# Two gate projections of the short convolution, moved from dense jobs into two groups of seven block products

## The chip, the core and the metric

The kernel runs on one core of one Trainium2 chip: one launch, with inputs and outputs in DRAM. The metric is the device time of the whole program in microseconds (us). TensorE (PE) multiplies, VectorE (DVE) and ScalarE (ACT) do elementwise work, GpSimd (POOL) does a little elementwise work and issues some transfers, SyncE (SP) issues most transfers. PEld is TensorE's weight load, which runs beside the matmuls.

## What is computed

One hybrid decoder layer over 1024 tokens with 16 meta tokens in front, width 1024, all in float32. Three causal mixers read the same normalised stream `xn` through one wide projection `w_in`; this is the reference, cut to what matters here:

```
xn   = rms_norm(x, norm_pre)
proj = xn @ w_in                      # split into ssd_*, sc_b, sc_c, sc_h, sc_g, dn_*, gate_logits
y_sc = sc_b * causal_depthwise_conv(sc_c * sc_h, sc_conv_w) * silu(sc_g)     # 3 taps
branch = einsum("btnw,nwd->btnd", [y_ssd, y_sc, y_dn], w_branch)
merged = sum over the 3 branches of sigmoid(gate_logits) * branch
out  = x + rms_norm(merged @ w_out, norm_post)
```

The change is about `sc_g` and `sc_b`, each a 1024 x 1024 x 1024 product followed by an elementwise multiplication.

## The kernel before

Activations lie with channels on the 128 partitions and tokens along the free dimension. Every float32 operand of a product is split into a high and a low part (ACT casts, DVE subtracts), and each product is three matmuls: high by high, high by low, low by high.

**Mixing stage.** 84 *dense jobs* each compute 128 output channels of `w_in` for all tokens: 8 blocks of k, three matmuls each, for two groups of 512 tokens (48 matmuls) or, where the result goes into a convolution, three groups of some 345 (72 matmuls). A job loads 512 KB of weights and splits them one job ahead (`split`, lines 159 to 167). Beside the jobs run the *mixes*: eight heads of the DeltaNet (`dn_mix`, tiles dm0 to dm7), whose last part is a chain over nine chunks in which every chunk takes three dependent steps (a matmul ks, then DVE's R; a matmul pn, then ACT's vn; a matmul su, then DVE's new state S), then eight pairs of SSD heads (`sd_mix`, tiles sm0 to sm7). Each mix is one *slot*; `weave` (line 192) hands out dense matmuls between the steps of a mix, `want * gap` columns of them, with a gap per kind of slot from the table `GAPS`, and then finishes the slot's jobs. A scheduler in the language then orders each engine's instructions. A DeltaNet slot holds the four jobs of the next head (q, k, v, z) and some jobs of the short convolution. The latter are four per 128 channels (`sc_jobs`, line 741): c and h (three groups each, then the three taps on DVE), g (SiLU on ACT, a multiplication on DVE) and bb (a multiplication on DVE, then stores of the rows to DRAM). The eight DeltaNet slots take 4, 3, 4, 3, 4, 4, 2 and 4 of these 32 jobs, and the last SSD slot ("sl") takes the last four. The last SSD slot also ends the row norm of the SSD branch: a matmul with the mean matrix (tiles sm7ms), a square root on ACT, a reciprocal of one row on DVE (line 908) and a store of that row (`rin_d`, line 909).

**Product stage.** The square products left are done by Strassen's scheme in Winograd's form: seven products of halves (512 x 512 x 512, 48 matmuls each, lines 1136 to 1138) in place of eight. A *group* is one such product, a *phase* one of its seven; phases are numbered n = 0 to 48 over seven groups (gate and branch for each of the three mixers, in the order 2, 1, 0, then the output). PSUM banks y and z hold the running sums; `finish` (line 1155) does the elementwise end of each quarter: a sigmoid for a gate group; a multiplication with the gate, and but for the first branch an addition to `merged`, for a branch group. For the next phase, each phase loads operand halves (`tr`), splits them into th and tl, and splits the weights w. The seven right operands of each product are sums of quarters that lie ready in DRAM; POOL makes them with accumulating transfers (`sums`, line 125), issued one by one, with a small copy (`tick`, line 1247) as a marker of the phase. `scale_tasks` (line 1218) applies the SSD row norm: it loads pieces `ys`, DVE multiplies them by the row `rin` (line 1232), and they are stored. In before its loads are on SP's queue and its stores on ACT's.

Order of work around the change: each engine works strictly in the order in which its instructions stand, and an instruction that waits holds everything behind it on that engine.

Of the kernel before, what the change touches and what calls it, by code (L numbers as in the profile page):

```python
# [12 lines left out]
ALU = mybir.AluOpType  # L13
# [26 lines left out]
GAPS = {"sm": 1.0, 8: 2.3, 7: 2.0, 6: 1.75, "s0": 2.0, "sd": 2.4, "sx": 2.0, "sg": 2.0, "sl": 2.6}  # L40
# [43 lines left out]
def hybrid_block(  # L84
# [40 lines left out]
    def sums(s, straight=None, ks=slice(0, HK)):  # L125

        o = {n: t[:, ks, :] for n, t in dict(opd[s], **(straight or {})).items()}
# [613 lines left out]
    def sc_jobs(t):  # L741
        n = f"sc{t}"
        tl = {}
        h0 = META - 2

        def c(w):
            tl["c"] = tmp(n + "c")
            yield from dense(w, xh, xl, three(h0), lambda o, c0, m: A.copy(tl["c"][:, c0:c0 + m], o), name=n + "c")

        def hh(w):  # L750
            ch = tl["c"]
            yield from dense(w, xh, xl, three(h0),
                             lambda o, c0, m: V.tensor_tensor(ch[:, c0:c0 + m], o, ch[:, c0:c0 + m], ALU.mult),
                             name=n + "h")
            acc = tl["a"] = big(n + "a", "sca", 1, SEQ)
            V.tensor_scalar(acc, ch[:, h0:h0 + SEQ], sc_cw(0, t), None, ALU.mult)
            for k in range(1, 3):
                V.scalar_tensor_tensor(acc, ch[:, h0 + k:h0 + k + SEQ], sc_cw(k, t), acc, ALU.mult, ALU.add)

        def g(w):  # L760
            gs = tmp(n + "g")
            yield from act_job(gs, n + "g")(w)
            V.tensor_tensor(tl["a"], tl["a"], gs[:, :SEQ], ALU.mult)

        def bb(w):
            acc = tl["a"]

            def use(o, c0, m):
                s = acc[:, c0 - META:c0 - META + m]
                j = (c0 - META) // HALF  # L770
# [205 lines left out]
    late = (lambda: (yield from chain(lambda: sums("dn"), lambda: sums("sc", ks=slice(0, HK - 1)))))()  # L976

    slot("dn", None, lambda: dn_jobs(0, dnt[0]))
    for h, n in enumerate((4, 3, 4, 3, 4, 4, 2, 4)):
        fs = [lambda h=h: dn_jobs(h + 1, dnt[h + 1])] if h < DN_H - 1 else [  # L980
            lambda: sdg_jobs(0, grps[0]), lambda: sd_jobs(0, sdt[0])]
        slot(4 + n, lambda h=h: beside(lambda: dn_mix(h, dnt[h]), early, 9), lambda n=n: sc_next(n), *fs)
    for t in range(KT):
# [3 lines left out]
        mix = lambda gens=gens: beside(lambda: chain(*gens), late, 7)  # L987
# [3 lines left out]
        fs.append((lambda t=t: sd_jobs(t + 1, sdt[t + 1])) if t < KT - 1 else lambda: sc_next(4))  # L991
# [163 lines left out]
    def finish(g, i, j, u):  # L1155
# [62 lines left out]
    def scale_tasks():  # L1218
        for i in range(2):
            for j in range(2):  # L1220
# [29 lines left out]

    g0 = groups[0]
# [7 lines left out]
    for n, (g, ph) in enumerate(steps):  # L1259
# [75 lines left out]
```

## Time and profile before

| | us |
|---|---|
| median of 3 runs (lowest, highest) | 1863.25 (1862.57, 1865.03) |
| profiled execution, its own time | 1867.32 |
| its span, first to last instruction | 1865.2 |
| PE busy / DVE busy / ACT busy / POOL busy | 1822.1 / 1272.1 / 829.4 / 200.4 |
| mean granted TensorE clock | 0.992 of full speed |

The profile is one execution. Matmuls overlap in the pipeline, so that the duration of one (some 390 ns at 512 columns) is longer than the distance from one start to the next; what a matmul costs the stream is that distance. "Idle before" is the time an engine stood still ahead of an instruction, with what ended it. A window of the profile gives each engine's busy time and the granted clock in a stretch.

### The profile page before, as it was taken

How to read it: one execution, taken by the hardware profiler on the slowest of the kernel's cores; microseconds unless marked ns; L12 is line 12 of the kernel's file. 1: busy time of each engine (PE TensorE's matmuls, PEld its weight loads, DVE VectorE, ACT ScalarE, POOL GpSimd, SP SyncE). 2: the span in 40 equal slices, each digit the busy share in tenths (PEclk: the TensorE clock that was granted, in tenths of full speed). 3: DMA queues.
4: the chain of work that ended last, by engine and by line, in shares of the span. 5: the costliest groups of instructions: out<-in, count | busy, mean ns of one | idle time of the engine just before them, and what ended most of it. 6: DMA issues, size and time to landing. Idle time of an engine off the chain costs nothing.

```text
span 1865.2 us, 27616 instructions
## 1 busy us (share of the span) xinstructions
PE 1822.1 (98%) x11115; PEld 1576.5 (85%) x11115; DVE 1272.1 (68%) x1874; ACT 829.4 (44%) x1343; POOL 200.4 (11%) x339
## 2 busy tenths in 40 slices
PE   6999999999999999999999999999989999999997
PEld 5988988888888889888888899888777888888886
DVE  5576674656766666575756887786757857867787
ACT  5442524344352342434334556453535455455454
POOL 3011112010120100101001121110000000000000
PEclk8999999999999999999999999999999999999999
DMA  5123244233342311111124465222776545755532
GB/s 154 49 68 118 76 104 112 68 114 102 91 108 63 91 52 41 46 58 46 40 75 112 127 147 150 78 80 94 248 249 212 155 164 144 232 184 158 192 102 91
DMA packets 153482, 214.23 MB, mean 115 GB/s; under 512 B 11169, under 2 KB 97374, under 8 KB 153226
## 3 DMA queue, kind: packets, MB, share of 16 engines
q1 hardware_dynamic: 135666, 160.02, 27.3%
q0 software_dynamic: 11632, 32.51, 8.5%
q10 hardware_dynamic: 6056, 19.93, 2.7%
q8 instruction: 87, 1.43, 0.3%
q14 instruction: 41, 0.34, 0.1%
HBM read 179.83 MB, written 64.07 MB: 131 GB/s over the span
## 4 chain that ended last, share of the span: by engine, by line
PE 86%; DVE 5%; DMA 4%; ACT 2%; issue 1%; POOL 1%; SPq 0%; DVEq 0%; ACTq 0%; POOLq 0%
PE py L1138 5%; PE py L1137 5%; PE py L1136 5%; PE pz L1138 4%; PE pz L1137 3%; PE pz L1136 3%; DMA ys<-y_sd 1%; DMA a__13752<-in_w_branch_dram 1%; DVE gt L1214 1%; DVE w L163 0%; DMA gain<-in_norm_pre_dram 0%; DMA sd_n<-ys 0%; DMA tr<-dn_n 0%; DVE dm7osq L734 0%; DMA x_t<-x_t 0%
## 5 line engine op out<-in xcount | busy, mean ns | idle before, releaser
L1138 PE MATMUL py<-th,w 128*128 128x512 f32 x432 | 168.9, 391 | 3.8 <-DVE w L1117 3.6
L1136 PE MATMUL py<-th,w 128*128 128x512 f32 x432 | 168.8, 391 | 0.0
L1137 PE MATMUL py<-tl,w 128*128 128x512 f32 x432 | 168.8, 391 | 0.0
L1101 DVE TENSOR_TENSOR tl<-tr,th 128x1024 fp32r<-128x1024 f32 x94 | 114.0, 1221 | 66.2 <-ACT th L1100 65.5
L1100 ACT CAST th<-tr 128x1024 fp32r<-128x1024 f32 x94 | 98.4, 1053 | 105.8 <-PE py L1138 44.2
L1138 PE MATMUL pz<-th,w 128*128 128x512 f32 x320 | 124.8, 390 | 3.5 <-DVE w L1117 2.8
L1136 PE MATMUL pz<-th,w 128*128 128x512 f32 x320 | 124.6, 389 | 0.0
L1137 PE MATMUL pz<-tl,w 128*128 128x512 f32 x320 | 124.5, 389 | 0.0
L163 DVE TENSOR_TENSOR w<-raw,w 128x1024 fp32r<-128x1024 f32 x84 | 103.4, 1231 | 14.3 <-ACT w L162 13.7
L1138 PEld LDWEIGHTS py<-th,w 128*128 128x128 f32 x432 | 81.5, 189 | 21.9 <-DVE w L1117 4.4
L162 ACT CAST w<-raw 128x1024 fp32r<-128x1024 f32 x84 | 88.1, 1048 | 21.4 <-PE sc2h L186 4.0
L1137 PEld LDWEIGHTS py<-tl,w 128*128 128x128 f32 x432 | 81.5, 189 | 17.1
L1136 PEld LDWEIGHTS py<-th,w 128*128 128x128 f32 x432 | 81.4, 188 | 16.9
L1138 PEld LDWEIGHTS pz<-th,w 128*128 128x128 f32 x320 | 60.1, 188 | 17.1 <-DVE w L1117 3.7
L1136 PEld LDWEIGHTS pz<-th,w 128*128 128x128 f32 x320 | 60.1, 188 | 12.7 <-ACT pz L1145 0.4
L1137 PEld LDWEIGHTS pz<-tl,w 128*128 128x128 f32 x320 | 60.1, 188 | 12.5
L1148 ACT COPY u<-py 128x1024 f32<-128x1024 f32 x30 | 30.4, 1015 | 52.4 <-PE py L1138 48.1
L1247 POOL COPY tick<-th 128x1 f32<-128x1 f32 x12 | 10.7, 890 | 354.1 <-ACT th L1100 354.1
L1161 DVE TENSOR_TENSOR u<-pz,u 128x1024 f32<-128x1024 f32 x30 | 36.5, 1218 | 7.6 <-PE pz L1138 7.6
L1167 ACT ACTIVATE gt<-u 128x1024 f32<-128x1024 f32 x14 | 14.8, 1060 | 26.0 <-DVE u L1161 22.7
L476 ACT ACT_TABLE_LOAD x18 | 23.1, 1283 | 4.5 <-PE sd3z L186 1.1
L245 PE MATMUL xp<-ident,xg 128*128 128x128 f32 (+1 forms) x72 | 10.9, 303 | 11.9 <-DVE xg L239 10.1
(1887 smaller groups left out, 5627.4 us busy)
## 6 DMA issues: line engine op xcount, KB each, us to landing
raw<-in_w_in_dram SPq DMA_DIRECT2D x84, 512.0 KB, 4.2
tr<-x_t SPq DMA_DIRECT2D x24, 512.0 KB, 4.9
tr<-x SPq DMA_DIRECT2D x10, 512.0 KB, 5.2
ys<-y_sd SPq DMA_DIRECT2D x16, 256.0 KB, 3.1
tr<-dn_t SPq DMA_DIRECT2D x8, 512.0 KB
tr<-sc_t SPq DMA_DIRECT2D x8, 512.0 KB, 3.9
tr<-sd_t SPq DMA_DIRECT2D x8, 512.0 KB, 5.6
tr<-wo_t SPq DMA_DIRECT2D x8, 512.0 KB, 4.6
```

Of the source, the lines that this page charges most:

```text
L162: A.copy(wh, raws[i])
L163: V.tensor_tensor(wl, raws[i], wh.bitcast(F32), ALU.subtract)
L476: lambda o, c0, n: A.activation(dst[:, c0 - META:c0 - META + n], o, fn), name=name)
L1100: A.copy(h, src)
L1101: V.tensor_tensor(l, src, h.bitcast(F32), SUB)
L1136: PE.matmul(o, lhsT=w[:, 0, k, cs], rhs=r1, start=fresh and k == 0, stop=False, skip_group_check=not fresh)
L1137: PE.matmul(o, lhsT=w[:, 0, k, cs], rhs=r2, start=False, stop=False, skip_group_check=not fresh)
L1138: PE.matmul(o, lhsT=w[:, 1, k, cs], rhs=r1, start=False, stop=k == HK - 1, skip_group_check=not fresh)
L1148: A.copy(t, g.ps["y", u])
L1161: V.tensor_tensor(k, t, k, ADD)
L1167: A.activation(quarter_tile(gate, "gt", i, j)[:, qs, :], t, AF.Sigmoid)
L1214: V.scalar_tensor_tensor(o, o, tot, fin["x", t][:, es], ALU.mult, ADD)
```

## The change

The jobs g and bb are gone, so that 16 of the 84 dense jobs are left out. The convolution of c times h is stored to a DRAM tensor `conv`, by quarters. The two gates become two groups of the product stage, "cg" (SiLU, times the convolution) and "cb" (times that), right behind the first gate and branch pair; there are nine groups and 63 phases now. In cg the parked quarters are loaded in phases 0, 3, 4 and 5. In cb the finished rows are stored by POOL, and POOL's sums of them follow in the next group, one per phase. The DeltaNet slots take 2, 2, 2, 2, 2, 2, 1, 1 jobs of the short convolution, the last SSD slot 2; a gap of 1.45 is new for a slot of five jobs. The loads and stores of `scale_tasks` are issued by POOL in program order, instead of by SP and ACT, and its steps are handed out from phase 9 instead of 7.

```diff
-GAPS = {"sm": 1.0, 8: 2.3, 7: 2.0, 6: 1.75, "s0": 2.0, ...
+GAPS = {"sm": 1.0, 8: 2.3, 7: 2.0, 6: 1.75, 5: 1.45, "s0": 2.0, ...
...
+    conv = {(i, j): dram.tile([P, HK, HALF], F32, name=f"conv{i}{j}") for i in range(2) for j in range(2)}
...
-        def g(w):
-            gs = tmp(n + "g")
-            yield from act_job(gs, n + "g")(w)
-            V.tensor_tensor(tl["a"], tl["a"], gs[:, :SEQ], ALU.mult)
-
-        def bb(w):
...
-                V.scalar_tensor_tensor(s, o, 1.0 if t // HK == j else -1.0, s, ALU.mult, ALU.mult)
-                for dst in quarters("sc", t // HK, j):
-                    (GP if t == KT - 1 else DMA).dma_start(dst[:, t % HK, :], s)
...
-        return (C_CC + t * P, c), (C_CH + t * P, hh), (C_CG + t * P, g), (C_CB + t * P, bb)
+            for j in range(2):
+                (GP if t == KT - 1 else DMA).dma_start(conv[t // HK, j][:, t % HK, :], acc[:, j * HALF:(j + 1) * HALF])
+
+        return (C_CC + t * P, c), (C_CH + t * P, hh)
...
-    late = (lambda: (yield from chain(lambda: sums("dn"), lambda: sums("sc", ks=slice(0, HK - 1)))))()
+    late = sums("dn")
...
-    for h, n in enumerate((4, 3, 4, 3, 4, 4, 2, 4)):
+    for h, n in enumerate((2, 2, 2, 2, 2, 2, 1, 1)):
...
-        fs.append((lambda t=t: sd_jobs(t + 1, sdt[t + 1])) if t < KT - 1 else lambda: sc_next(4))
+        fs.append((lambda t=t: sd_jobs(t + 1, sdt[t + 1])) if t < KT - 1 else lambda: sc_next(2))
...
+    POST = ("cg", "cb")
     for b in ORDER:
         for kind in "gb":
             groups.append(Group(kind, b))
+        if b == ORDER[0]:
+            for kind in POST:
+                groups.append(Group(kind, 0))
...
+        elif g.kind == "cg":
+            A.activation(t, t, AF.Silu)
+            cv = gate[i, j][:, qs, :]
+            V.tensor_tensor(cv, t, cv, ALU.mult)
+        elif g.kind == "cb":
+            cv = gate[i, j][:, qs, :]
+            V.scalar_tensor_tensor(cv, t, 1.0 if i == j else -1.0, cv, ALU.mult, ALU.mult)
+            for dst in quarters("sc", i, j):
+                GP.dma_start(dst[:, qs, :], cv)
...
-                        DMA.dma_start(t[:, k, :], y_sd[n + k][:, js])
+                        background(GP, t[:, k, :], y_sd[n + k][:, js])
...
-                        A.dma_start(dst[:, 2 * u:2 * u + 2, :], t)
+                        background(GP, dst[:, 2 * u:2 * u + 2, :], t)
...
-        if q == 2 and 7 <= n < 23:
+        if q == 2 and 9 <= n < 25:
             next(scale, None)
...
+        if g.kind == POST[0] and ph in PARKED:
+            ij = PARKED[ph]
+            gate.pop(ij, None)
+            DMA.dma_start(quarter_tile(gate, "gt", *ij), conv[ij])
```

How it moves instructions, at three places. The first is ACT at the end of the mixing stage. sqa are the squared rows of the SSD norm, sm7ms the mean matmul, sc7g the eighth g job's result, rin_d the stored reciprocal, w_00 the first weights of the product stage. Before:

```order
L907 ACTIVATE sqa_1_12167<-sm7ms_13306,eps 128x512
L907 ACTIVATE sqa_2_12168<-sm7ms_13316,eps 128x512
L476 ACT_TABLE_LOAD
L476 ACTIVATE sc7g<-sc7g_13302 128x512
L909 DMA rin_d_117<-sqa_1_12167 1x512
L476 ACTIVATE sc7g<-sc7g_13348 128x512
L909 DMA rin_d_117<-sqa_2_12168 1x512
L1116 CAST w_00_13446<-a__13444 128x1024
```

and now:

```order
L895 ACTIVATE sqa_1_11352<-sm7ms_12478,eps 128x512
L895 ACTIVATE sqa_2_11353<-sm7ms_12488,eps 128x512
L897 DMA rin_d_121<-sqa_1_11352 1x512
L897 DMA rin_d_121<-sqa_2_11353 1x512
L1109 CAST w_00_12512<-a__12510 128x1024
```

The norm's square roots and row stores stand directly ahead of the product stage's first cast; the g job between them is gone (on DVE likewise: its two reciprocals, L896, now stand directly ahead of that cast's subtraction, where the splits and multiplications of the last two jobs stood).

The second is PE in the chunk chain of DeltaNet head 6 (su and ks are two successive steps, pn the third; o is the head's output, off the chain; dn7 is a dense job). Before, with six dense jobs in the slot:

```order
L702 MATMUL dm6su_9266<-dm6vn_9256,dm6kd 128x128
L711 MATMUL dm6o_9161<-dm6PT_8546,dm6vn_9256 128x128
L185 MATMUL dn7z_9243<-xl,w_9059 128x512
L186 MATMUL dn7z_9243<-xh,w_9059 128x512
L690 MATMUL dm6ks_9287<-dm6S_9268,dn6k 128x128
L184 MATMUL dn7z_9243<-xh,w_9059 128x512
L185 MATMUL dn7z_9243<-xl,w_9059 128x512
L186 MATMUL dn7z_9243<-xh,w_9059 128x512
L695 MATMUL dm6pn_9294<-dm6R_9289,dm6Y_9125 128x128
```

and now, with five:

```order
L705 MATMUL dm6su_8729<-dm6vn_8721,dm6kd 128x128
L714 MATMUL dm6o_8680<-dm6PT_8025,dm6vn_8721 128x128
L188 MATMUL dn7v_8746<-xl,w_8631 128x346
L189 MATMUL dn7v_8746<-xh,w_8631 128x346
L693 MATMUL dm6ks_8738<-dm6S_8731,dn6k 128x128
L713 MATMUL dm6o_8680<-dm6row,dm6S_8731 128x128
L187 MATMUL dn7v_8746<-xh,w_8631 128x346
L188 MATMUL dn7v_8746<-xl,w_8631 128x346
L698 MATMUL dm6pn_8750<-dm6R_8740,dm6Y_8543 128x128
```

Between two steps stand two or three dense matmuls as before, but of 346 columns instead of 512.

The third is the scaled rows, of which SP issued the loads before (ys is a piece, y_sd the rows in DRAM, a__13678 a block of branch weights, tr an operand half):

```order
L1090 DMA tr_51_13676<-x_t_86 128x1024
L1228 DMA ys_14017<-y_sd_73 128x512
L1228 DMA ys_14169<-y_sd_74 128x512
L1228 DMA ys_14169<-y_sd_75 128x512
L1223 DMA rin_14325<-rin_d_116 128x512
L1228 DMA ys_14327<-y_sd_72 128x512
L1228 DMA ys_14327<-y_sd_73 128x512
L1042 DMA a__13678<-in_w_branch_dram 128x4x512
```

and POOL issues loads and stores now:

```order
L763 DMA conv_119<-sc7a 128x512
L126 DMA ys_13223<-y_sd_72 128x512
L126 DMA ys_13223<-y_sd_73 128x512
L126 DMA sd_102<-ys_13223 128x1024
L126 DMA ys_13377<-y_sd_74 128x512
L126 DMA ys_13377<-y_sd_75 128x512
L126 DMA sd_102<-ys_13377 128x1024
L126 DMA ys_13531<-y_sd_72 128x512
```

Only the rows' loads of `rin` are left on SP. On POOL a piece's load stands behind the store of the piece before it. DVE's eight multiplications stand where they stood: from the preparation of phase 3 to that of phase 8.

## Rows read from the trace of the kernel before

**Rows 1.** The page: span, busy time by engine, chain that ended last.

```profile
span 1865.2 us, 27616 instructions
PE 1822.1 (98%) x11115; PEld 1576.5 (85%) x11115; DVE 1272.1 (68%) x1874; ACT 829.4 (44%) x1343; POOL 200.4 (11%) x339
...
PE 86%; DVE 5%; DMA 4%; ACT 2%; issue 1%; POOL 1%; SPq 0%; DVEq 0%; ACTq 0%; POOLq 0%
```

**Rows 2.** Windows of DeltaNet slots: heads 0 to 5, head 5, 6, 7.

```profile
core 0: us, PE busy (x) PEld busy (x) DVE busy (x) ACT busy (x) POOL busy (x), PEclk, DMA share, GB/s
87.70:790.30 702.60, 696.58 (x4945) 617.84 (x4944) 448.23 (x761) 274.34 (x572) 98.05 (x171) 1.00 0.30 83
670.10:790.30 120.20, 119.30 (x841) 105.69 (x840) 74.69 (x127) 44.31 (x94) 13.34 (x26) 1.00 0.18 49
790.30:888.20 97.90, 97.40 (x698) 82.80 (x696) 63.32 (x118) 43.61 (x91) 13.32 (x25) 1.00 0.17 49
888.20:1016.60 128.40, 127.21 (x894) 112.00 (x891) 84.36 (x134) 51.01 (x104) 13.49 (x21) 1.00 0.25 69
```

**Rows 3.** Timeline of PE, dense matmuls: start, duration, instruction.

```profile
55.73 0.32 PE L184 MATMUL dn0q<-xh,w 128*128 128x342 f32 x1
55.89 0.32 PE L185 MATMUL dn0q<-xl,w 128*128 128x342 f32 x1
...
118.55 0.40 PE L184 MATMUL sc0g<-xh,w 128*128 128x512 f32 x1
118.78 0.40 PE L185 MATMUL sc0g<-xl,w 128*128 128x512 f32 x1
```

**Rows 4.** Timeline of PE, first matmuls of two successive phases.

```profile
1441.03 0.39 PE L1136 MATMUL pz<-th,w 128*128 128x512 f32 x1
...
1451.91 0.39 PE L1136 MATMUL py<-th,w 128*128 128x512 f32 x1
```

**Rows 5.** Timeline of the chunk chain of head 6.

```profile
866.41 0.41 PE L695 MATMUL dm6pn<-dm6R,dm6Y 128*128 128x128 f32 x2
...
867.36 0.46 PE L702 MATMUL dm6su<-dm6vn,dm6kd 128*128 128x128 f32 x2
...
868.35 0.40 PE L690 MATMUL dm6ks<-dm6S,dn6k 128*128 128x128 f32 x2
...
869.30 0.28 PE L695 MATMUL dm6pn<-dm6R,dm6Y 128*128 128x128 f32 x1
```

**Rows 6.** Timelines at the end of mixing: PE at the slot's start.

```profile
1252.41 0.40 PE L184 MATMUL sc7c<-xh,w 128*128 128x342 f32 x1
```

**Rows 7.** There, DVE, with idle time before and what ended it.

```profile
1283.03 0.51 DVE L753 TENSOR_TENSOR sc7c<-sc7h,sc7c 128x342 f32<-128x342 f32 x1 [1.28 <-PE sc7h L186]
...
1288.44 1.22 DVE L163 TENSOR_TENSOR w<-raw,w 128x1024 fp32r<-128x1024 f32 x1
1289.58 6.54 DVE L908 RECIPROCAL sqa<-sqa 1x512 f32<-1x512 f32 x2
1296.06 1.15 DVE L763 TENSOR_TENSOR sc7a<-sc7a,sc7g 128x1024 f32<-128x1024 f32 x1
```

**Rows 8.** There, ACT.

```profile
1296.16 0.25 ACTq L909 DMA_DIRECT2D rin_d<-sqa  x1
1306.36 2.00 ACT L1116 CAST w<-a__13444 128x1024 fp32r<-128x1024 f32 x2 [10.54 <-PE sc7b L186]
```

**Rows 9.** There, PE.

```profile
1307.46 0.50 PE L1136 MATMUL py<-xh,w 128*128 128x512 f32 x1 [1.13 <-ACT w L1116]
1308.72 0.50 PE L1138 MATMUL py<-xh,w 128*128 128x512 f32 x1 [0.53 <-DVE w L1117]
```

**Rows 10.** Windows: just after that, and a later gate and branch stretch.

```profile
1309.20:1312.70 3.50, 3.50 (x11) 2.69 (x10) 3.50 (x4) 0.10 (x1) 0.00 (x0) 0.52 1.00 401
...
1571.60:1647.80 76.20, 76.20 (x338) 63.10 (x337) 62.22 (x55) 35.22 (x35) 8.18 (x8) 1.00 0.73 205
```

**Rows 11.** Timeline of PE, first matmuls of phases 5 and 9.

```profile
1364.83 0.39 PE L1136 MATMUL py<-th,w 128*128 128x512 f32 x1
...
1419.27 0.39 PE L1136 MATMUL py<-th,w 128*128 128x512 f32 x1
```

**Rows 12.** Waits: engine, line, waited for: us in total, times, longest.

```profile
DVE ys L1232 <- DMA ys<-y_sd: 14.8, 6, 6.1
...
PE dm1ms L731 <- ACT dm1oh L722: 3.4, 1, 3.4
```

**Rows 13.** Transfers of ys, and POOL's of sc: issue in ns min/median/max, landing.

```profile
L1228 SPq DMA_DIRECT2D ys<-y_sd x16: 319/429/965, 1322.8 to 1395.6; - x16
...
DMA to landing us min/median/max: 3.1/3.1/6.5
...
L123 POOL DMA_DIRECT2D sc_t<-sc x2: 828/850/871, 1343.2 to 1372.4; - x2
L773 POOL DMA_DIRECT2D sc<-sc7a x1: 573/573/573, 1307.4 to 1307.4; - x1
...
DMA to landing us min/median/max: 7.2/8.5/9.2
```

More of the change, by code (lines that the diff above doesn't have):

```diff
@@ L39 @@
 HK = KT // 2
-GAPS = {"sm": 1.0, 8: 2.3, 7: 2.0, 6: 1.75, "s0": 2.0, "sd": 2.4, "sx": 2.0, "sg": 2.0, "sl": 2.6}
+GAPS = {"sm": 1.0, 8: 2.3, 7: 2.0, 6: 1.75, 5: 1.45, "s0": 2.0, "sd": 2.4, "sx": 2.0, "sg": 2.0, "sl": 2.6}
 class Block:
@@ L123, in background, with sums @@
         tc.keep_in_program_order(eng.dma_start(*args, **kw))
-    def sums(s, straight=None, ks=slice(0, HK)):
-        o = {n: t[:, ks, :] for n, t in dict(opd[s], **(straight or {})).items()}
+    def sums(s, straight=None):
+        o = dict(opd[s], **(straight or {}))
         for dst, a, b in (("t1", None, "11"), ("t3", None, "22"), ("t2", "t1", "22"), ("t4", "t2", "n21")):
@@ L758, in hh @@
                 V.scalar_tensor_tensor(acc, ch[:, h0 + k:h0 + k + SEQ], sc_cw(k, t), acc, ALU.mult, ALU.add)
-        def g(w):
-            gs = tmp(n + "g")
-            yield from act_job(gs, n + "g")(w)
-            V.tensor_tensor(tl["a"], tl["a"], gs[:, :SEQ], ALU.mult)
-        def bb(w):
[L766 to L770, printed above, removed]
-                V.scalar_tensor_tensor(s, o, 1.0 if t // HK == j else -1.0, s, ALU.mult, ALU.mult)
-                for dst in quarters("sc", t // HK, j):
-                    (GP if t == KT - 1 else DMA).dma_start(dst[:, t % HK, :], s)
-            yield from dense(w, xh, xl, TWO, use, name=n + "b")
-        return (C_CC + t * P, c), (C_CH + t * P, hh), (C_CG + t * P, g), (C_CB + t * P, bb)
+            for j in range(2):
+                (GP if t == KT - 1 else DMA).dma_start(conv[t // HK, j][:, t % HK, :], acc[:, j * HALF:(j + 1) * HALF])
+        return (C_CC + t * P, c), (C_CH + t * P, hh)
     def sdg_jobs(g, grp):
@@ L986, in hybrid_block @@
             lambda t=t, g=g: sd_mix(t, grps[g], sdt[t])]
-        mix = lambda gens=gens: beside(lambda: chain(*gens), late, 7)
+        mix = lambda gens=gens: beside(lambda: chain(*gens), late, 9)
         fs = []
@@ L1052, in __init__ @@
             self.blk, self.raw, self.t, self.w, self.ps, self.st = {}, {}, {}, {}, {}, {}
-            self.wsrc = {"g": cols_of(w_in, C_G + b * D), "b": cols_of(w_branch[b])}.get(kind)
-            self.ops = opd["x" if kind == "g" else ("sd", "sc", "dn")[b]]
+            self.wsrc = {"g": cols_of(w_in, C_G + b * D), "b": cols_of(w_branch[b]), "cg": cols_of(w_in, C_CG),
+                         "cb": cols_of(w_in, C_CB)}.get(kind)
+            self.ops = opd[("sd", "sc", "dn")[b] if kind == "b" else "x"]
             if kind == "o":
@@ L1233, in scale_tasks @@
                     for dst in quarters("sd", i, j):
-                        A.dma_start(dst[:, 2 * u:2 * u + 2, :], t)
+                        background(GP, dst[:, 2 * u:2 * u + 2, :], t)
                     yield 0
-    scale, sd_sums, sc_sums = scale_tasks(), sums("sd"), sums("sc", ks=slice(HK - 1, HK))
+    scale, sd_sums, sc_sums = scale_tasks(), sums("sd"), sums("sc")
     tick = c1.tile([P, 1], F32, name="tick", tag="tick")
+    sc0 = 7 * (2 + len(POST))
     def extra(n, q):
-        if q == 2 and 7 <= n < 23:
+        if q == 2 and 9 <= n < 25:
             next(scale, None)
-        side = sc_sums if n in range(4, 16, 2) else sd_sums if n in range(24, 36, 2) else None
+        side = sc_sums if n in range(sc0 + 1, sc0 + 7) else sd_sums if n in range(sc0 + 8, sc0 + 20, 2) else None
         if q == 3 and side is not None:
@@ L1248, in extra @@
             next(side, None)
+    PARKED = {0: (0, 0), 3: (1, 1), 4: (1, 0), 5: (0, 1)}
     g0 = groups[0]
```

## The prediction

> **What bounds the kernel now.** I read the page first: PE is busy in 98% of the span and makes up 86% of the chain that ended last [rows 1]. So a change is worth what it takes off PE's stream, less the places where PE then stands still. Since a mean hides stages, I then cut the span into slots and phases with the windows and looked for PE's waits. In the DeltaNet slots PE is busy 99% of the time, DVE 62% in head 5 (74.7 of 120.2) and 65% in head 6 [rows 2]. The product stage, where nothing disturbs it, takes 1451.91 - 1441.03 = 10.88 us for a phase of 48 matmuls, 0.227 each [rows 4]. PE stands still in two places only that matter here: at the seam between the stages, and in phases 5 to 8.
>
> The profiled execution took 1867.32 us, 2.1 more than its span and 4.1 more than the median of the three runs; I work out a difference on its rows and take it from the median, 1863.25.
>
> **Part by part.**
>
> *Dense jobs out of the DeltaNet slots.* A dense matmul of 512 columns costs the stream 0.23 us and one of 342 costs 0.16 [rows 3]. So a g or bb job is 48 x 0.234 = 11.2 us and a c or h job 72 x 0.158 = 11.4. The slots confirm it: head 5 with eight jobs takes 120.2, head 6 with six takes 97.9, so 11.15 per job [rows 2]. Heads 0 to 5 will have six jobs each. Head 6 shows what such a slot takes; with c and h where it has g and bb it is 98.2. That makes 589.2 for 702.6. Head 6 goes from six to five jobs (g and bb out, one c in), 97.9 - 22.4 + 11.4 = 86.9. Head 7 loses c, g and bb: 128.4 - 33.8 = 94.6.
>
> *What the filler hid.* One step of the chunk chain needs 0.94 to 0.99 us from its matmul to the next step's (867.36 - 866.41, 868.35 - 867.36, 869.30 - 868.35) [rows 5]; in this round little but the dense matmuls lies between, so I take 0.95 as the least. In the changed order of head 6, many steps have two matmuls of 346 columns between them, 2 x 0.16, and one or two small ones of 0.11: 0.54 us in place of 0.95. I counted the 24 steps of each head and added what is missing to 0.95: 2.5 us in the old head 6 (which are in its 97.9), 5.7 in the new head 6, 4.9 in the new head 7 (1.6 in the old), 5.1 in head 0, 3.7 in head 2; heads 1, 3, 4 and 5 have the old head 6's pattern. Against the sums above that is 3.2 + 3.3 + 2.6 + 1.2 = 10.3 more. As a bound from below, PE's profile shows hardly any wait in the old chain, so it could be 0; from above, the triangular inversion ahead of the chain could lose as much again, 20. I take the counted value. Together: heads 0 to 5 to 593.0 (-109.6), head 6 to 90.1 (-7.8), head 7 to 97.9 (-30.5).
>
> *The seam.* The last slot starts at 1252.41 [rows 6] and the end of job h, its second, releases DVE at 1283.03, 30.6 later [rows 7]. From there DVE works without a pause until 1296.1: taps, norm, two reciprocals of 6.54 together. Today PE spends that time on jobs g and bb, and the product stage begins only when bb ends: ACT casts at 1306.36 [rows 8], PE starts at 1307.46 and gets on at 1308.72 [rows 9], 2.36 after the cast begins. In the changed order nothing is left behind h but four matmuls of the mean. The cast and the subtraction of the first weights stand behind both reciprocals and both row stores (1296.16 for the second today [rows 8]). DVE's stretch shortens by one weight split, 1289.58 - 1288.44 = 1.14, so the cast starts at 13.1 - 1.1 + 0.3 = 12.3 after the end of h and PE gets on at 14.7. The slot and seam take 30.6 + 14.7 = 45.3 in place of 1308.72 - 1252.41 = 56.3: -11.0, where the two jobs alone would give -22.5. The bounds are the cast right at the end of h (-22.5, if the scheduler's order did not bind) and the norm's chain late by one more square root and table load (-9).
>
> The granted clock fell to 0.52 from 1309.2 to 1312.7, after idle times of only 1.13 and 0.53 us [rows 9, 10]; 3.5 us at the lower level (1.2 GHz) cost 1.7. A longer standstill pays this once too, perhaps sooner: +1, between 0 and 3. The Trainium skill says the same of PE's pauses ("TensorE: Matmul & The Clock Gate", section "HAM oscillation — how this bites in real kernels"): a wait on other work sends the array back to half rate, and the next stretch starts cold. By that rule the seam costs its wait and a cold start behind it, which the trace agrees with, at 0.52.
>
> *Two groups more.* 14 phases at 10.88: +152.3. What could hold PE there is DVE. A cg quarter costs it one multiplication more than a gate group does, a branch group two operations more, and a stretch of 76.2 us made of later gate and branch phases has DVE at 62.2 and PE at 76.2 without a gap [rows 10]. The parked quarters are 4 MB over cg beside some 11 MB of operands and weights, 15 MB in 76 us, about 200 GB/s, no more than the 205 that this stretch moved. The 14 phases therefore count in full and nothing beside. If DVE did bind in cb and cg, it would be one or two us a phase, at most 20.
>
> *Scaled rows through POOL.* Phases 5 to 8 take 1419.27 - 1364.83 = 54.4 where four undisturbed ones take 43.5: 10.9 lost [rows 11]. DVE waits 14.8 for pieces ys [rows 12], and SP, held by these loads, brings the branch weights late. The change takes them off SP and ACT, so weights and casts no longer queue behind them. But on POOL a piece's loads now stand behind the store of the piece before. A round is store, load, load: three issues of 0.57 at the least and a landing of 3.1 as from SP, 4.8; at the most four issues of 0.85 and a landing of 8.5, 11.9 [rows 13]. The eight pieces stand in DVE's order over six phases, 65.3 us. I take 7, nearer the loads' row than that of the accumulating transfers: 56 us, which fits, but the first four stand closer together than 7. I leave 7 of the 10.9 in: -4 (between -10.9 and +20).
>
> *Sum.* -109.6 - 7.8 - 30.5 - 11.0 + 152.3 + 1 - 4 = -9.6, so 1863.25 - 9.6 = 1854, rounded. Whatever else the change moves (16 weight loads and splits, fewer stores in the mixing stage, POOL's six sums of sc out of it) lies beside PE.
>
> **Rivals.**
>
> *A, stalls hidden.* The scaled rows stop disturbing (7 more) and the chain loses half of what I counted (5 more): 1842. For it: PE's small waits in the old chain are few. Against it: the changed order has 0.54 us in step after step.
>
> *B, slower: POOL's round binds.* If a round takes over 8.2 us, eight of them no longer fit in the six phases, and DVE, which has the splits of the next phase queued behind each piece, holds PE for the excess. At 11.9 that is 95 - 65 = 30 us in place of 10.9 lost: 1854 + 4 + 19 = 1877. It decides from 10.2 us a round on, where the excess of 16.5 eats the 5.6 that the other terms gain. For it: POOL's transfers in this stage landed after 7.2 to 9.2 us, against 3.1 for SP's loads [rows 13]. Against it: two of these accumulate, and the third is a store in the seam's rush (401 GB/s there [rows 10]). The Trainium skill speaks for it ("DMA: Bandwidth & Descriptors", section "SWDGE vs HWDGE vs iDMA"): transfers from GpSimd have their descriptors written by software, into SBUF state from which VectorE can lock it out, and those from SP or ACT do not. By that rule the piece would come later the busier DVE is, and DVE waits for it; no row here separates that from the load on the DMA engines.
>
> *C, the slots do not shrink so far.* Head 1 once held PE for 3.4 us at its end, where the norm's matmul waited for ACT [rows 12]. Should shorter slots all end so, with 9 us more in eight heads, it is 1863, no change. Against it: head 6, the shortest so far, has 0.5 us of idle PE in all (97.9 less 97.4).
>
> **Chances.** My forecast, 1847 to 1859: 0.55. A: 0.2. B: 0.12. C: 0.13. What a measurement can tell from no change is 0.2%, 3.7 us. Faster by more, under 1859.5: nearly all of the forecast, A and a little of C, 0.76. Within: most of C, a little of the forecast and B's low end, 0.13. Slower: 0.11. The range takes A's value and C's and leaves most of B out: 1841 to 1864.
>
> **What would show it.** Slots of heads 1, 3, 4 and 5 at 98 us; heads 6 and 7 near 90 and 98, with PE waits on ACT's vn and DVE's S that before has not; PE idle some 13 us ahead of the first product matmul, ended by ACT or DVE, with the clock near 0.5 after it; 10.88 us for nearly all of the 63 phases; the rest of the lost time in phases 3 to 9, with DVE waiting for ys. I am wrong if the seam is hidden, if slots of six jobs stay over 105, or if the lost time around phases 3 to 9 is over 17.

## The result, and the profile of the changed kernel

The changed kernel takes 1877.55 us (median of 4 runs, 1873.60 to 1878.58) and the kernel before 1862.91 beside it: a ratio of 1.0074 (95% interval 1.0059 to 1.0089). It is slower by some 14 us (14.6 between the medians), where 9 faster were forecast. The profiled executions stand 10.3 apart (1877.63 to 1867.32), the spans 10.7; the profiled execution of before was 4.4 above the median of 1862.91, which is the rest, and no row shows where in it those lie. What follows is worked out between the two spans.

The page of the changed kernel, to be held against [rows 1]:

```profile
span 1875.9 us, 27654 instructions
PE 1814.0 (97%) x11019; PEld 1563.0 (83%) x11019; DVE 1340.0 (71%) x1930; ACT 893.9 (48%) x1397; POOL 219.9 (12%) x369
```

PE is busy 8.1 us less in a span that is 10.7 longer: 19 us more in which it stands. Windows of the changed kernel, columns as in [rows 2]: heads 0 to 5, head 3, head 6, head 7, last slot with the seam, the half-clock stretch at the seam, the product stage:

```profile
88.40:694.00 605.60, 595.93 (x4467) 529.21 (x4465) 413.89 (x735) 270.50 (x561) 100.41 (x171) 0.99 0.31 87
395.30:494.90 99.60, 98.43 (x747) 87.85 (x745) 67.81 (x122) 45.66 (x94) 17.16 (x30) 1.00 0.44 109
694.00:786.20 92.20, 89.58 (x675) 76.78 (x673) 63.10 (x116) 40.26 (x89) 12.85 (x25) 1.00 0.14 41
786.20:885.40 99.20, 96.14 (x726) 83.45 (x725) 77.64 (x126) 46.90 (x97) 15.07 (x21) 1.00 0.27 75
1120.15:1163.82 43.67, 33.13 (x223) 29.80 (x221) 32.33 (x52) 16.44 (x24) 4.84 (x8) 0.87 0.45 147
1152.60:1169.70 17.10, 8.22 (x16) 5.03 (x17) 15.71 (x12) 5.99 (x7) 2.25 (x4) 0.50 0.93 319
...
1163.82:1865.47 701.65, 691.56 (x3024) 570.22 (x3024) 508.78 (x464) 349.30 (x371) 40.50 (x58) 0.99 0.60 189
```

Heads 0 to 5 fell by 97.0 where 109.6 was predicted, head 6 by 5.7 (7.8), head 7 by 29.2 (30.5), last slot with seam by 11.4 (11.0). The product stage took 547.17 before and grew by 154.5, where groups, clock and scaled rows were put at 152.3 + 1 - 4 = 149.3. The start is 0.7 later and the other SSD slots 1.1 shorter. Sum: +0.7 - 97.0 - 5.7 - 29.2 - 1.1 - 11.4 + 154.5 = +10.8.

What PE waits for in the changed kernel (in total, times, longest), but for one wait of 10.3 at the start of the program, where before has one of 9.4:

```profile
PE pz L1129 <- ACT pz L1138: 8.1, 1, 8.1
PE py L1129 <- ACT w L1109: 7.0, 1, 7.0
PE sm7ms L893 <- ACT sm7sh L890: 2.1, 2, 1.8
PE dm1ms L734 <- ACT dm1oh L725: 1.9, 1, 1.9
PE py L1131 <- DVE w L1110: 1.9, 1, 1.9
```

The first and the last lie in phase 7, the second and third at the seam, the fourth at the end of head 1. Timeline of all engines around phase 7:

```profile
1240.79 1.08 POOL L126 DMA_DIRECT2D ys<-y_sd  x2
1246.83 0.75 DVE L1234 SCALAR_TENSOR_TENSOR ys<-ys,nsnw,rin 128x512 f32<-128x512 f32 x1 [3.46 <-DMA ys<-y_sd]
...
1249.67 0.54 POOL L126 DMA_DIRECT2D sd_n<-ys  x1 [7.80 <-DVE ys L1234]
1250.20 1.08 POOL L126 DMA_DIRECT2D ys<-y_sd  x2
...
1251.69 0.50 PE L1131 MATMUL py<-th,w 128*128 128x512 f32 x1 [1.90 <-DVE w L1110]
1257.79 0.75 DVE L1234 SCALAR_TENSOR_TENSOR ys<-ys,snw,rin 128x512 f32<-128x512 f32 x1 [4.89 <-DMA ys<-y_sd]
...
1265.14 0.80 PE L1129 MATMUL pz<-th,w 128*128 128x512 f32 x1 [8.14 <-ACT pz L1138]
```

POOL issues a piece's loads (1250.20) only behind the store of the piece before (1249.67), which waits for DVE; they land some 7 us later, and the next scaling starts at 1257.79, 11.0 after that of 1246.83. DVE has its next phase's splits queued behind it. Phase 7 takes 1265.14 - 1243.74 = 21.4 us, and phase 8, partly at half clock, 12.64: against two phases of 10.88, 12.3 lost. The tail of head 1, all engines:

```profile
283.33 0.53 POOL L126 DMA_DIRECT2D x_t<-x_t  x1 [7.34 <-DMA x_t<-x]
283.86 0.60 ACT L722 ACTIVATE dm1osq<-dm1o 128x512 f32<-128x512 f32 x1 [0.81 <-PE dm1o L714]
...
288.92 1.00 POOL L126 DMA_DIRECT2D x_t<-x_n  x1 [5.05 <-DMA x_t<-x_t]
289.58 1.63 POOL L723 TENSOR_TENSOR dm1osq<-dm1osq,dn1q 128x512 f32<-128x512 f32 x1
291.24 0.62 ACT L725 CAST dm1oh<-dm1osq 128x512 fp32r<-128x512 f32 x1 [3.38 <-POOL dm1osq L723]
...
291.91 0.50 PE L734 MATMUL dm1ms<-dm1oh,cmeanr 128*128 128x512 f32 x1 [1.92 <-ACT dm1oh L725]
```

ACT has the square ready at 284.5. POOL's addition starts at 289.58, since ahead of it in POOL's order stands an accumulating DMA of the x sums that waits for the one before. PE runs at half clock for 6.8 us from 292.44 on. This wait is the 3.4 of [rows 12]: before has it too, behind the same order on POOL. And the seam, all engines:

```profile
1155.86 6.54 DVE L896 RECIPROCAL sqa<-sqa 1x512 f32<-1x512 f32 x2
...
1159.23 3.45 ACTq L897 DMA_DIRECT2D rin_d<-sqa  x2
1162.72 1.99 ACT L1109 CAST w<-a__12510 128x1024 fp32r<-128x1024 f32 x2 [5.21 <-DVE sqa L896]
...
1163.82 0.80 PE L1129 MATMUL py<-xh,w 128*128 128x512 f32 x1 [7.03 <-ACT w L1109]
```

As predicted, the casts stand behind two reciprocals and both row stores.

### The profile page after: what moved, and what is told of

The parts are those of the page before. It is cut to its first block, busy times and chain, and to the rows that moved or that the text cites. A ratio compares the mean times of both kernels' runs of the same rounds, so it can differ in the third digit from the quotient of the medians.

```text
span 1875.9 us, 27654 instructions
## 1 busy us (share of the span) xinstructions
PE 1814.0 (97%) x11019; PEld 1563.0 (83%) x11019; DVE 1340.0 (71%) x1930; ACT 893.9 (48%) x1397; POOL 219.9 (12%) x369
## 3 DMA queue, kind: packets, MB, share of 16 engines
q1 hardware_dynamic: 124978, 173.65, 29.2%
## 4 chain that ended last, share of the span: by engine, by line
PE 85%; ACT 4%; DVE 4%; DMA 3%; issue 2%; POOL 1%; SPq 0%; ACTq 0%; DVEq 0%; POOLq 0%
PE py L1129 6%; PE py L1131 6%; PE py L1130 6%; PE pz L1129 5%; PE pz L1130 5%; PE pz L1131 5%; DMA ys<-y_sd 1%; DMA dm2row<-cum_d 1%; DVE gt L1216 1%; ACT L470 0%; DMA gain<-in_norm_pre_dram 0%; DMA rin<-rin_d 0%; DMA raw<-in_w_in_dram 0%; PE sm L364 0%; DMA x_t<-x_t 0%
## 5 line engine op out<-in xcount | busy, mean ns | idle before, releaser
L1131 PE MATMUL py<-th,w 128*128 128x512 f32 x560 | 218.1, 389 | 1.9 <-DVE w L1110 1.9
L1130 PE MATMUL py<-tl,w 128*128 128x512 f32 x560 | 217.9, 389 | 0.0
L1129 PE MATMUL py<-th,w 128*128 128x512 f32 x560 | 217.9, 389 | 0.0
L1094 DVE TENSOR_TENSOR tl<-tr,th 128x1024 fp32r<-128x1024 f32 x122 | 148.1, 1221 | 88.5 <-ACT th L1093 87.6
L1093 ACT CAST th<-tr 128x1024 fp32r<-128x1024 f32 x122 | 127.7, 1053 | 124.9 <-PE py L1131 60.0
L1129 PE MATMUL pz<-th,w 128*128 128x512 f32 x416 | 162.7, 391 | 8.1 <-ACT pz L1138 8.1
L1130 PE MATMUL pz<-tl,w 128*128 128x512 f32 x416 | 162.5, 391 | 0.0
L1131 PE MATMUL pz<-th,w 128*128 128x512 f32 x416 | 162.3, 390 | 0.0
L1131 PEld LDWEIGHTS py<-th,w 128*128 128x128 f32 x560 | 105.1, 188 | 24.4 <-DVE w L1110 2.3
L1129 PEld LDWEIGHTS py<-th,w 128*128 128x128 f32 x560 | 105.1, 188 | 21.8
L1130 PEld LDWEIGHTS py<-tl,w 128*128 128x128 f32 x560 | 105.1, 188 | 21.8
L1129 PEld LDWEIGHTS pz<-th,w 128*128 128x128 f32 x416 | 78.5, 189 | 24.9 <-ACT pz L1138 8.6
L166 DVE TENSOR_TENSOR w<-raw,w 128x1024 fp32r<-128x1024 f32 x68 | 83.7, 1231 | 17.3 <-ACT w L165 17.1
L1131 PEld LDWEIGHTS pz<-th,w 128*128 128x128 f32 x416 | 78.5, 189 | 16.4
L1250 POOL COPY tick<-th 128x1 f32<-128x1 f32 x12 | 12.5, 1043 | 154.4 <-ACT th L1093 154.4
```

The costliest lines, as they stand in the source:

```text
L166: V.tensor_tensor(wl, raws[i], wh.bitcast(F32), ALU.subtract)
L1093: A.copy(h, src)
L1094: V.tensor_tensor(l, src, h.bitcast(F32), SUB)
L1129: PE.matmul(o, lhsT=w[:, 0, k, cs], rhs=r1, start=fresh and k == 0, stop=False, skip_group_check=not fresh)
L1130: PE.matmul(o, lhsT=w[:, 0, k, cs], rhs=r2, start=False, stop=False, skip_group_check=not fresh)
L1131: PE.matmul(o, lhsT=w[:, 1, k, cs], rhs=r1, start=False, stop=k == HK - 1, skip_group_check=not fresh)
```

## The experiments

Each ratio is to the kernel before, run on the same chip, with its 95% interval.

**e1: the scaling operations later.** The eight pieces are pinned in DVE's order to where the program writes them.

```diff
-V.scalar_tensor_tensor(t[:, k, :], t[:, k, :], w, r, ...)
+tc.keep_in_program_order(V.scalar_tensor_tensor(t[:, k, :], t[:, k, :], w, r, ...))
```

> The changed kernel with the eight scaling operations on VectorE pinned to where the program writes them, one piece in two phases from phase 10 on; in the changed kernel they stand in phases 3 to 9, some 9 us apart. Theory 1 (a piece's load stands behind the store of the piece before on GpSimd's queue, a round takes 8 to 11 us, and VectorE waits in order with the next phase's splits behind it): with 21.8 us a round VectorE never waits for ys, phases 7 and 8 take 10.88 like the others, the 12.3 us lost there go: 1865 (1863 to 1867). Theory 2 (phases 7 and 8 are late for another reason, the new groups' weights or the parked quarters): no change, 1877.

Measured: 1865.23 us, ratio 1.0009 (1.0000 to 1.0018), 12.3 less than the changed kernel. Timeline of POOL, and the window of phases 5 to 8:

```profile
1284.25 0.54 POOL L126 DMA_DIRECT2D sd<-ys  x1 [123.91 <-DVE ys L1234]
...
1306.00 0.54 POOL L126 DMA_DIRECT2D sd<-ys  x1 [20.14 <-DVE ys L1234]
```

```profile
1223.67:1267.19 43.52, 43.52 (x193) 36.04 (x192) 30.74 (x27) 23.41 (x24) 0.00 (x0) 1.00 0.40 136
```

A piece now has 21.8 us, DVE no longer waits for ys, and four phases take 4 x 10.88 = 43.52. Theory 1 holds.

**e2: the scaled rows back on SP and ACT.** The one part of the change undone.

```diff
-background(GP, t[:, k, :], y_sd[n + k][:, js])
+DMA.dma_start(t[:, k, :], y_sd[n + k][:, js])
-background(GP, dst[:, 2 * u:2 * u + 2, :], t)
+A.dma_start(dst[:, 2 * u:2 * u + 2, :], t)
```

> The changed kernel with the scaled rows' loads back on SyncE and their stores back on ScalarE, all else as changed. Theory 1 (VectorE's order asks for pieces faster than any queue brings them; the queue hardly matters): the stage loses about what it lost before, 10.9, against 12.3 now, 1876 (1873 to 1879). Theory 2 (GpSimd's round of store, load, load is the whole price): the loss in phases 3 to 9 falls under 4 us, 1868.

Measured: 1872.85 us, ratio 1.0049 (1.0034 to 1.0064). Waits of DVE, 1155 to 1300, and the window of phases 5 to 8:

```profile
DVE ys L1234 <- DMA ys<-y_sd: 11.6, 3, 6.1
...
DVE a__12744 L1116 <- DMA a__12818<-in_w_branch_dram: 5.5, 1, 5.5
```

```profile
1223.44:1274.04 50.60, 46.41 (x194) 36.87 (x192) 39.86 (x39) 24.48 (x25) 0.00 (x0) 0.97 0.72 248
```

Between the two theories: four phases take 50.6, so 7.1 are still lost, and DVE waits for ys and for a weight block. POOL's queue costs 4.7 us here (with the spread of both runs, 1 to 9); the rest is DVE's order, as e1 shows.

**e3: the kernel before with its scaled rows on POOL.** The edit of e2 the other way round.

> The kernel before with only the scaled rows moved to GpSimd. Theory 1: the loss of 10.9 us around phases 5 to 8 stays within 3 us of that, 1863 (1860 to 1867). Theory 2 (GpSimd's round is the price of the changed kernel): 5 us or more above, 1868 to 1880. What the prediction said (-4, of the weights no longer queued behind the loads): 1859.

Measured: 1864.06 us, ratio 1.0006 (0.9996 to 1.0016), no change that can be told. The phases around 5 to 8 run undisturbed and phases 14 to 17 lose 8.0 instead: DVE's order changes with the queue. Theory 1's time holds, and the 4 us that the prediction expected are not there. (Between the profiled executions the product stage is 4.4 shorter, 542.7 to 547.2, but this one stands 3.0 below its median and that of before 4.4 above, so that says nothing.)

**e4: the side steps at other places.**

```diff
-beside(lambda: dn_mix(h, dnt[h]), early, 9)
+beside(lambda: dn_mix(h, dnt[h]), early, 11)
```

> The changed kernel with the side steps of the heads (rounding pieces of x, negated weights and their sums by accumulating DMA) taken at every 11th step of the mixing in place of every 9th. By the order of GpSimd's queue only one DMA of the x sums, one that waits for no other, then stands between the two osq additions of head 1, where three stand now. Theory 1 (head 1's tail is held by those DMAs: the addition waits on GpSimd behind an issue that waits for the sum before, TensorE stands 2.4 us and then runs 6.8 us at half clock, 3.4 us more): heads 1 and 2 get shorter by 5 to 6 us together, 1872. Theory 2 (the wait only moves to another head): no change, 1877.

Measured: 1878.83 us, ratio 1.0084 (1.0067 to 1.0102): no gain. Heads 1 and 2 are shorter by 4.1, but head 4 is 4.4 longer, as theory 2 has it. Timeline of SP and DVE there:

```profile
545.82 0.90 SPq L490 DMA_DIRECT2D dm5row<-cum_d  x1
...
559.67 0.16 DVE L496 TENSOR_TENSOR dm5F<-dm5row,ncum 16x16 f32<-16x16 f32 x1 [4.50 <-DMA dm5row<-cum_d]
```

The load of the next head's decay row was issued at 545.82, beside two sums of the output weights, and DVE got it at 559.67, 13.9 later; the first head's row, issued before any of these sums, landed in 3.4. In that run the wait only moved; whether its cause is the same is for e5.

**e5: e1 and e4, and the sums of the output weights out of the heads** (into the SSD slots, behind those of dn).

```diff
-late = sums("dn")
+late = (lambda: (yield from chain(lambda: sums("dn"), lambda: sums("wo", wo_straight))))()
```

> The kernel of e1 (1865.2) with the side steps at every 11th step of the mixing, and the sums of the output weights taken out of the heads into the SSD slots, behind those of dn. Theory 1 (the standstills in head 1, and in e4 in head 4, are made by these accumulating DMAs: GpSimd's queue held by them in the one, a row broadcast slowed by them in the other): both go, heads 0 to 5 get shorter by 4 to 7 us, 1860 (1858 to 1862). Theory 2 (shorter slots wait for something at their ends in any case): a wait of the same size turns up elsewhere, 1865.

Measured: 1861.49 us, ratio 0.9997 (0.9987 to 1.0006), against 1.0009 for e1: the two intervals overlap, so that the gain is read from the profile. The longest wait in heads 0 to 5 is 1.1, and heads 0 to 6 take 692.8, against 697.8 in the changed kernel and 699.5 in e1. Both standstills go, the slots of six jobs stay at 99.5 to 101.1, and theory 1 holds.

**e6: the reciprocals out of the seam** (on e1). The root is stored, and the broadcast row is inverted in the product stage.

```diff
-V.reciprocal(sqa[b][0:1, :], sqa[b][0:1, :])
+tc.keep_in_program_order(V.reciprocal(r, r))      # in scale_tasks, behind the load of r
```

> The kernel of e1 with the reciprocals of the SSD norm's rows out of the seam: the square root is stored, and the four broadcast pieces (128x512) are inverted in the product stage, pinned in front of their pieces. Theory 1 (as the prediction had it: the first weight casts stand behind two reciprocals of 6.54 us together and the row stores on ScalarE): the cast starts some 4.5 us sooner, TensorE's idle time of 7.0 falls under 3, and less of phase 0 runs at half clock, 1860 (1858 to 1862). Theory 2 (the seam is bound by the weights' loads or the norm's chain): 1865. Four reciprocals of 3.35 us lie in phases where VectorE has 25 % to spare and cost nothing; if they do, it is up to 1870.

Measured: 1858.50 us, ratio 0.9981 (0.9972 to 0.9990). Timeline of PE:

```profile
1158.41 0.80 PE L1128 MATMUL py<-xh,w 128*128 128x512 f32 x1 [2.14 <-ACT w L1108]
```

The idle time of 7.0 is down to 2.1, slot and seam take 38.8 in place of 43.7, and the four reciprocals of 128x512 cost nothing beside PE: every phase behind phase 1 but the last takes 10.88. Theory 1 holds, but for the half clock: phase 0 loses 3.6, where it lost 2.8 in e1.

**e7: three jobs in the last slot** (on e1).

```diff
-for h, n in enumerate((2, 2, 2, 2, 2, 2, 1, 1)):        # and sc_next(2) in the last slot
+for h, n in enumerate((2, 2, 2, 2, 2, 2, 1, 0)):        # and sc_next(3); GAPS for 4 jobs: 1.2
```

> The kernel of e1 with one short-convolution job fewer in head 7's slot (four in all) and one more in the last slot (three). Theory 1 (the last slot is as long as its mixing and norm, 43.7 us with the seam for two jobs of 11.3, so a third fills time that TensorE stands idle; head 7's slot gets shorter by 9): the seam stage grows by 3 to 5, 1860 (1858 to 1862). Theory 2 (what is behind the last job, taps and reciprocals, sets the start of the product stage, and the third job moves it by its full length): the seam grows by 11, 1867.

Measured: 1855.78 us, ratio 0.9966 (0.9954 to 0.9978). Timeline of PE:

```profile
1151.09 0.50 PE L1129 MATMUL py<-xh,w 128*128 128x512 f32 x1 [1.14 <-ACT w L1109]
...
1155.12 0.80 PE L1131 MATMUL py<-xh,w 128*128 128x512 f32 x1 [3.30 <-DVE w L1110]
```

The last slot starts at 1107.0, so slot and seam take 44.0 with three jobs, where they took 43.7 with two. Phase 0 pays 3.7 back, with DVE at the taps: the third job costs 4.1 of its 11. That is theory 1, though the time came out 2 us under its range.

**e8: another placement of the dense matmuls** (on e1).

```diff
-GAPS = {..., 6: 1.75, ...}
+GAPS = {..., 6: 2.0, ...}
```

> The kernel of e1 with the planner's number for slots of six jobs at 2.0 in place of 1.75: more dense matmuls between the mixing's early steps, fewer at the end. Theory 1 (the 1.4 us by which such a slot exceeds the 98.2 of the prediction are small waits that hang on where the dense matmuls stand): heads 0 to 5 change by over 3 us, and for the worse if the chunk chain at the end is the thin place: 1870. Theory 2 (what matters is how many dense matmuls there are, not where): within 2 us, 1865.

Measured: 1863.06 us, ratio 1.0007 (0.9998 to 1.0017): no change in the whole, as theory 2 has it, but its profile shows two things. Windows of heads 0 to 6 and of head 4:

```profile
88.60:784.00 695.40, 678.00 (x5141) 606.54 (x5139) 483.26 (x850) 316.13 (x656) 109.65 (x196) 0.99 0.29 81
504.80:602.90 98.10, 97.44 (x745) 87.73 (x744) 68.98 (x122) 43.61 (x93) 15.33 (x29) 1.00 0.27 73
```

An undisturbed slot of six jobs takes 98.1, what the prediction had. And heads 1 and 3 now stop PE for 7.87 and 3.24, with half clock after each; timeline of SP and DVE in head 1, and of POOL in head 3:

```profile
241.16 0.58 SPq L490 DMA_DIRECT2D dm2row<-cum_d  x1
...
257.04 1.37 DVE L496 TENSOR_TENSOR dm2F<-dm2row,ncum 16x16 f32<-16x16 f32 x3 [10.29 <-DMA dm2row<-cum_d]
```

```profile
462.46 0.52 POOL L126 DMA_DIRECT2D wo_t<-wo_t  x1 [12.98 <-DMA wo_t<-in_w_out_dram]
```

In head 1 it is the decay row again, issued at 241.16 among the x sums and used 15.9 later. In head 3 it is POOL's queue: a copy waits 12.98 for the sum before it, and behind it stand POOL's masks of the next head; ACT waits for these ahead of head 3's vn, and PE for vn. So placement moves the slots by the size that theory 1 had (heads 0 to 6 took 699.5 in e1, 695.4 here) with the other sign, and the two standstills took back most of what it gained; e11 tries it without them.

**e9: the kernel before with the two mends,** pinned pieces as in e1 and the sums as in e5.

> The kernel before with the two mends that do not belong to the change: the eight scaling operations pinned to where the program writes them (as in e1, here with the loads still on SyncE), and the side steps at every 11th step with the sums of the output weights in the SSD slots (as in e5). It tells what the change is worth where neither standstill is there. Theory 1 (the standstills belong to the scaled rows and the sums and not to the change): the 10.9 us of phases 5 to 8 and the 3.4 + 3.4 in head 1 go, 1863 - 17 = 1846 (1844 to 1850), some 15 under e5, so that the change itself costs time where all stalls are mended. Theory 2 (the fuller slots of the kernel before had hidden all but the product stage's loss): 1852.

Measured: 1846.96 us, ratio 0.9910 (0.9893 to 0.9926). PE never waits over 1.2 us between 60 and 1300, and phases 5 to 8 take 10.88 each, with the loads on SP. The two standstills were worth 16.5 in the kernel before; with both mended the changed kernel (e5) is 14.5 behind (16 by the ratios), where it is 14.6 behind with neither. So the standstills alone do not explain why the change is slower.

**e10: e1, e5, e6 and e7 together.**

> The changed kernel with e1, e5, e6 and e7 together. If the gains lie in different places they add up: 1865.2 - 3.7 - 6.7 - 9.4, less what e6 and e7 both took off the same idle time in the seam (some 4): 1849 (1847 to 1852). Rival: with the seam filled by the third job the reciprocals no longer matter, and e6 adds nothing: 1852 (1851 to 1854).

Measured: 1852.11 us, ratio 0.9942 (0.9927 to 0.9957). The two forecasts meet at 1852, so the profile decides, and the rival holds: with three jobs in the last slot the taps (3.30 of idle PE, as in e7) end last and the reciprocals no longer matter.

**e11: all sums out of the heads, and placement 2.0** (on e10).

```diff
-GAPS = {..., 6: 1.75, ...}          # late: dn, wo, at every 9th step
+GAPS = {..., 6: 2.0, ...}           # late: x, dn, wo, at every 7th step; early: at every 9th again
```

> The kernel of e10 with the sums of x in the SSD slots too (side steps at every 9th in the heads and every 7th there) and the planner's number for six jobs at 2.0. Theory 1 (in e8 the undisturbed six-job slots took 98.1, as predicted, and only the x and wo sums stopped heads 1 and 3): all six slots of heads 0 to 5 take 98 to 99, some 8 us less than in e10, 1841 (1838 to 1844). Theory 2 (12 more accumulating DMAs in the SSD slots hold the masks there on GpSimd): the SSD slots grow by 5 or more, and e10's time is kept, 1848.

Measured: 1837.06 us, ratio 0.9859 (0.9845 to 0.9874): the fastest here, 26 us under the kernel before. Heads 1 to 5 take 95.4 to 98.4, head 0 takes 106.9, and the SSD slots no more than in e10: theory 1's mechanism, but 4 us under its time and 1 under its range.

**e12: e11 at 1.75 again.**

> The kernel of e11 with the planner's number for six jobs back at 1.75, so that it differs from e10 in the sums of x alone and from e11 in that number alone. Between e10 and e11 the heads' slots (start of dm0 to start of sm0) fell from 787.3 to 771.0. Theory 1 (the placement of the dense matmuls makes the small waits of the six-job slots, and the x sums cost only what can be seen as standstills, 2 to 4 us): 1849 (1847 to 1851), slots 784, six-job slots at 99.5. Theory 2 (the x sums were the price, the planner's number only moves the borders of the slots): 1839 (1836 to 1841), slots 773.

Measured: 1849.54 us, ratio 0.9922 (0.9905 to 0.9938). Windows of e12: heads 0 to 5, head 6, head 4, and all eight.

```profile
88.20:687.00 598.80, 592.19 (x4466) 526.74 (x4464) 414.09 (x735) 270.02 (x561) 89.50 (x159) 1.00 0.21 67
687.00:779.30 92.30, 89.64 (x676) 76.85 (x673) 63.18 (x116) 40.22 (x89) 12.84 (x25) 1.00 0.14 41
487.90:587.40 99.50, 98.34 (x746) 87.82 (x744) 68.13 (x122) 43.81 (x92) 13.48 (x26) 1.00 0.18 51
...
88.20:872.20 784.00, 771.75 (x5822) 681.30 (x5820) 547.34 (x968) 354.34 (x744) 118.20 (x206) 1.00 0.21 64
```

The same windows of e11, but for head 4:

```profile
86.70:681.90 595.20, 592.10 (x4514) 533.93 (x4512) 427.71 (x740) 274.32 (x567) 85.46 (x159) 1.00 0.22 68
681.90:764.90 83.00, 81.62 (x627) 69.81 (x626) 56.05 (x111) 41.87 (x90) 13.65 (x26) 1.00 0.13 39
...
86.70:857.70 771.00, 763.77 (x5821) 681.30 (x5819) 553.49 (x968) 359.95 (x749) 115.85 (x206) 1.00 0.21 65
```

The same work, no wait over 1.1 us in either, and 13.0 us between them from where the dense matmuls stand. Of these, 8.0 lie in PE's busy time (771.75 to 763.77), since a matmul of some 390 ns reaches past the 230 to the next start [rows 3], and a short wait hides in that. Theory 1 holds.

## Why the prediction was wrong

**Seam and groups: right.** Slot and seam took 43.7 us where 45.3 were predicted up to where PE goes on; the seam was bound by the two reciprocals and the row stores, as e6 shows. Undisturbed phases took 10.88 in every run, cg and cb too. What I did not draw from it: a slot with idle PE takes another job for a third of its price (e7).

**What the filler hid: half its size.** Without standstills (e12) heads 0 to 6 take 598.8 + 92.3 = 691.1. The clean slots of the prediction, 6 x 98.2 + 86.9, are 676.1. So the thinner filler cost 15.0 there, where I had counted 3.8 + 3.2 = 7.0 in the chunk chain; the bound from above, 20, held it. It is many small waits (PE is busy 98.34 of 99.5). Head 0 is 2.5 longer, as counted (2.6); heads 1 to 5 are 7.1 longer, where I had counted 1.2, and head 6 5.4 (3.2). In the six-job slots the chain was not the place. Windows ahead of the chain and of the chain, head 6 of before, then head 4 of e12:

```profile
790.31:851.06 60.75, 60.75 (x478) 50.74 (x475) 46.69 (x89) 22.96 (x59) 5.54 (x18) 1.00 0.20 62
851.06:880.71 29.65, 29.15 (x175) 24.79 (x175) 14.93 (x27) 16.18 (x25) 5.19 (x5) 1.00 0.14 36
```

```profile
487.94:550.15 62.21, 61.55 (x524) 55.69 (x522) 51.45 (x93) 23.15 (x60) 5.71 (x19) 1.00 0.22 65
550.15:579.91 29.76, 29.26 (x175) 24.85 (x175) 14.94 (x27) 16.18 (x25) 5.20 (x5) 1.00 0.14 36
```

The chain is the same; the slot loses ahead of it, in the part that my sum put at nothing and only the bound named. Nor is it a price of having fewer dense matmuls: with the other placement (e11) it is 678.2 - 676.1 = 2.1. The step that failed is "Head 6 shows what such a slot takes". That slot of before had six jobs, but slots of eight, planned at 2.3, ahead of it; that this is why it ran clean is argued, not shown; that the placement makes the loss is shown (e12 against e11).

**Head 1's standstill: counted as gone without a reason.** By putting 6 x 98.2 for all six heads I left out the 3.4 of [rows 12] and the half clock after it, which are in the 702.6. They stayed: 697.8 (the changed kernel) - 691.1 (e12) = 6.7. Slot lengths, as rival C supposed, are not the cause: the long slots of before have it, and it goes, in slots of either length, when the sums stand elsewhere (e5, e9). What does it is the accumulating DMAs, on POOL's queue and beside the row loads (e4, e8).

**Scaled rows: wrong sign.** I took 7 us for POOL's round and 7 us left over. Rounds of 9 to 11 us stood where DVE's order asked for a piece every 9 or so, and 12.3 were lost, with 0.2 more in phase 5. In the changed kernel the move to POOL costs 4.7 (e2), in the kernel before nothing that can be told (e3). So rival B named a mechanism that is there, and its time of 1877 was met only by the sum with the rest: its excess was 1.6 over the 10.9 of before, not 19. That the whole came out at B's 1877 is luck. Neither side of the forecast had that DVE's order, and not the queue, was the thing to mend: pinned late, the pieces cost nothing from POOL (e1) or from SP (e9).

**The sum.** The filler 8.0 more, head 1 6.7, head 7 1.3, the product stage 5.2, and 0.7 - 1.1 - 0.4 elsewhere: 20.4, which leads from -9.6 to +10.8. On the medians 4 more come from the profiled execution of before. None of the prediction's signs of being wrong came (six-job slots of 99.5 to 103.2, 12.5 lost in phases 3 to 9): the miss is made of terms of 5 to 8 us each, too small to trip one.

**What the change is worth.** With the standstills mended on both sides and nothing else, the changed kernel loses (e5 against e9, ratios 0.9997 and 0.9910). e12 also has what only the changed kernel was given, the reciprocals and a third job at the seam, and the x sums moved: it stands at 1849.5 against 1847.0 for e9 (ratios 0.9922 and 0.9910), nothing gained. With the dense matmuls placed for the shorter slots (e11) it is 0.9859 / 0.9910 = 0.9949, some 9 us faster. That this is near the forecast is luck, since the forecast had none of these mends. Whether the kernel before would gain from another placement too was not tried; PE hardly waits there, but 8 of the 13 us between e11 and e12 did not show as waits either.

## What to carry to other kernels

When work is taken out of a stage, the numbers that placed it (here one planner constant) were set for the old amount: price the stage from slots with the same neighbours, and retune before judging the change. A stall that the profile of before shows is still there afterwards unless the change removes its cause. Where an in-order engine waits for a transfer, move the waiting instruction before moving the transfer.

## What the runs showed of the hardware

An accumulating DMA on POOL's queue holds POOL's arithmetic too: the addition in head 1 started 5 us after its input was there, behind an issue that waited 5.05 for the DMA before it. A row load broadcast to 128 partitions landed in 3.4 us for the first head; where DVE waited for one with no such sums in the heads (e11, e12), it had it 4.9 to 5.8 us after the issue, and beside such sums only 13.9 and 15.9 us after it (e4, e8).

The granted clock fell to 0.5 for 6.8 us after PE had stood 1.92 us in head 1, and for 17 us around the seam, 8.9 of which PE stood still. The Trainium skill ("TensorE: Matmul & The Clock Gate", section "HAM oscillation — how this bites in real kernels") says of matmuls that waited for transfers that the wait sent the array back to half rate and the next stretch started cold. These stretches agree, with waits for other engines.
